# Down projection: when the weight differences are formed, when raw buffers are released, and where the third weight buffers lie

## The chip, the core and the metric

The kernel runs on one core of one Trainium2 chip. The metric is the device time of one execution in microseconds. Three runs of the kernel before gave 825.61, 826.12 and 826.38 us; their median is 826.12 us. Profiles are of one further execution, taken by the hardware profiler.

## The reference

One layer of a hybrid decoder: an attention sub-layer (two mixers, merged by gates) and a channel sub-layer, a gated MLP with a causal convolution of width 3. The change lies in the last product of the channel sub-layer, the down projection of a 512 x 2816 activation with a 2816 x 1024 weight:

```python
D_MODEL = 1024
SEQ = 512
D_FF = 2816

def conv_ffn(h, w_up, conv_w, conv_b, w_down):
    u = h @ w_up
    s = u.shape[1]
    up = jnp.pad(u, ((0, 0), (CONV_WIDTH - 1, 0), (0, 0)))
    c = conv_b + conv_w[0] * up[:, 0:s]
    for j in range(1, CONV_WIDTH):
        c = c + conv_w[j] * up[:, j:j + s]
    val, gate = jnp.split(c, 2, axis=-1)
    return (jax.nn.silu(gate) * val) @ w_down
...
        x = x + (merged @ w_out[l]).astype(x.dtype)
        h2 = rmsnorm(x, ffn_norm_g[l])
        x = x + conv_ffn(h2, w_up[l], conv_w[l], conv_b[l], w_down[l]).astype(x.dtype)
```

## The kernel before

All large products are made of float32r parts. A float32 operand x is rounded by ScalarE into a high part (`whi`) and VectorE subtracts to get a low part (`wlo = x - whi`); a product is then three matmuls: high by high, low by high, high by low.

The down projection is a 2 x 2 block product in Winograd's form with seven block products instead of eight, numbered 1 to 7. Blocks of the activation are 256 tokens by 1408 columns, blocks of the weight 1408 by 512. The 1408 rows are eleven rows of 128, taken in six chunks `CH` (two rows each, but one in the fifth). An *item* (j, c, n) is product j on the n rows from c. There are 42 items in three stretches: products 1, 5, 6 chunk by chunk (in the last chunk 1, 6, 5), then 7 and 3, then 2 and 4. One item of two rows is 12 matmuls of 512 columns: two halves of 128 tokens, each four with `whi` and two with `wlo`. The banks are `ps_a` (products 1 and 2), `ps_b` (5 and 3) and `ps_mm` (6, 7 and 4). Where a product follows another in the same bank, the sums of the first are copied out by ScalarE (`ev`) and added to by VectorE first.

The operand on the weight side is a raw block for products 1, 3 and 2, and a *difference* for the others, made by VectorE on float32 tiles of 128 x 1024:

- product 5: raw 5 less raw 1, in place;
- product 6: raw 6 less product 5's operand, into the tile T (T2 in the code);
- product 7: raw 3 less raw 7, in place;
- product 4: raw 2 less T, into T.

`load_next` (L1499) loads raw blocks of `w_down` through SP's queue into six places: three tiles `raw` and three slices of `hA`, an older buffer that the up projection's convolution uses until its end. `prepare` (L1572) makes one item ready: `weights` (L1537) forms the operand, and with it any difference, and `parts` (L1518) rounds and subtracts it. The pairs `whi`/`wlo` rotate over three buffers; every third item uses `whi3`/`wlo3`, which lie in the pool "down" together with T. This pool opens where the up projection's operands (`hh2`, `hl2`) lay. `AHEAD = 2`: item k + 2 is prepared ahead of the matmuls of item k. In the second and third stretches the activation operand of products 3 and 4 is rounded and subtracted too (`Sb`), after the weight's.

Within the down projection TensorE, VectorE and ScalarE run in the order in which the code is written (a manual schedule); SP's queue is ordered by the scheduler. The last lines of the up projection and the first item are outside of it. `users` holds for each place how many items must be ready before it is loaded again; before the change this is the number of items up to the end of the chunk, for all blocks of the chunk alike.

```python
        for k in range(len(items)):
            while len(ready) < min(k + 1 + AHEAD, len(items)):
                prepare()
            ...
            while load_next():
                pass
            product(k)
```

Of the kernel before, what the change touches and what calls it, by code (L numbers as in the profile page):

```python
# [12 lines left out]
F32 = mybir.dt.float32  # L13
F32R = mybir.dt.float32r
I32 = mybir.dt.int32
AF = mybir.ActivationFunctionType
ALU = mybir.AluOpType
# [66 lines left out]
def hybrid_block(ctx: ExitStack, tc: tile.TileContext, A: dict, out: bass.AP):  # L84
    nc = tc.nc
# [16 lines left out]
    def pool(name, side="left"):  # L102
        cm = tc.tile_pool(name=name, bufs=1, side=side)
        return cm, cm.__enter__()
# [8 lines left out]
    def mmb():  # L113
        return bank("mm", 4)
# [13 lines left out]
    def act(o, i, f=AF.Copy, **kw):  # L128
        sc.activation(o, i, f, **kw)  # L129

    def tt(o, a, b, op):
        v.tensor_tensor(o, a, b, op=op)  # L132
# [32 lines left out]
    for name in ("rwkv_mu", "rwkv_w0", "rwkv_a0", "rwkv_k_k", "rwkv_k_a", "rwkv_r_k", "rwkv_ln_g", "rwkv_ln_b"):  # L165
        r0, n = ROWS[name]
# [173 lines left out]
    with tc.manual_schedule(engines={getattr(mybir.EngineType, e) for e in ("PE", "Activation", "DVE", "Pool")}):  # L340
# [3 lines left out]
        hi = wp.tile([128, KT, 128], F32R, name="whi", tag="whi", bufs=2)  # L344
        lo = wp.tile([128, KT, 128], F32R, name="wlo", tag="wlo", bufs=2)
# [22 lines left out]
        r0, n = ROWS["rwkv_mu"]  # L368
# [45 lines left out]
    def dense_fm(xh, xl, kt=KT):  # L414
        return run(dense_fm_g(xh, xl, kt))
# [213 lines left out]
    for k in range(31):  # L629
        m, n = 31 - k, k + 1  # L630
# [7 lines left out]
    def dense_tok_g(n, xh, xl, kt=KT, halves=False, ends=False):  # L638
# [32 lines left out]
        for j, ks in enumerate(tiles[:-2]):  # L671
            parts = [(ks, wnext(len(ks), n))]
            for ts_ in ([range(2), range(2, NT)] if halves and j == 0 else [range(NT)]):
                yield from passes(parts, ts_)
# [420 lines left out]
    at_cm, at = pool("att")  # L1095
# [321 lines left out]
    with tc.manual_schedule(engines=KTS):  # L1417
        for t in range(NT):
            qs = slice(128 * t, 128 * t + 128)
            p = mmb()  # L1420
# [43 lines left out]
    def conv(p, f, i):  # L1464
        c = cgv[:, i]
        act(c, p, AF.Identity, scale=cw[:, 2, f:f + 1], bias=cw[:, 3, f:f + 1])
        stt(c[:, 1:], p[:, :-1], cw[:, 1, f:f + 1], c[:, 1:])
        stt(c[:, 2:], p[:, :-2], cw[:, 0, f:f + 1], c[:, 2:])
        return c

    def sums(i, lf, rt):
        l0, l1, r0, r1 = lf[:, 0:256], lf[:, 256:512], rt[:, 0:256], rt[:, 256:512]
        s1, s2, s3 = (tmp[:, j] for j in range(3))
        tt(s3, l0, l1, ALU.subtract)
        tt(s1, l1, r1, ALU.add)
        tt(s2, s1, l0, ALU.subtract)
        tt(s4[:, i], r0, s2, ALU.subtract)
        for w, x in zip(split, (l0, s1, s2, s3)):
            act(w[:, 0, i], x)
            tt(w[:, 1, i], x, w[:, 0, i].bitcast(F32), ALU.subtract)  # L1480
# [4 lines left out]
    def places():  # L1485
        yield from (0, 1, 2, 3)
        while True:
            yield from (0, 1, 2, 4, 5, 3)

    items, fetch = [], []  # L1490
    for js, last, froms in (((1, 5, 6), (1, 6, 5), ((1, 0, 0), (5, 0, 1), (6, 1, 1))),
                            ((7, 3), (7, 3), ((7, 0, 1), (3, 1, 1))), ((2, 4), (2, 4), ((2, 1, 0),))):
        for c, n in CH:
            items += [(j, c, n) for j in (last if c + n == NFH else js)]
            fetch += [(*f, c, n, len(items)) for f in froms]

    raws, turns3, turn, place, start, users = {}, itertools.count(), places(), [], [], [0] * 6

    def load_next():  # L1499
        if not start:  # L1500
            start.append(next(slots) % 3)
            place.append(next(turn))
        i = place[0]
        if not fetch or users[i] > len(ready) or (i > 3 and not T2):
            return False
        j, kh, fh, c, n, users[i] = fetch.pop(0)
        place[0] = next(turn)
        if i < 3:
            raw = wp.tile([128, n, 512], F32, name="raw", tag=f"raw{(start[0] + i) % 3}", bufs=1)
        else:  # L1510
            o = {3: 2048, 4: 0, 5: 1024}[i]
            raw = hA[:, o:o + 512 * n].rearrange("p (k n) -> p k n", k=n)
        r0 = 128 * (NFH * kh + c)
        nc.sync.dma_start(raw, w_down[r0:r0 + 128 * n, 512 * fh:512 * fh + 512].rearrange("(k p) n -> p k n", p=128))
        raws[j, c] = raw
        return True

    def parts(x, n):  # L1518
        if next(turns3) % 3 < 2:
            hi = wp.tile([128, n, 512], F32R, name="whi", tag="whi", bufs=2)  # L1520
            lo = wp.tile([128, n, 512], F32R, name="wlo", tag="wlo", bufs=2)
        else:
            hi, lo = (dn.tile([128, n, 512], F32R, name=k, tag=k) for k in ("whi3", "wlo3"))
        act(hi, x)
        tt(lo, x, hi.bitcast(F32), ALU.subtract)
        return hi, lo

    done = {}

    def difference(c):  # L1530
        if ("T1", c) not in done:
            x = raws[5, c]
            tt(x, x, raws[1, c], ALU.subtract)
            done["T1", c] = x
        return done["T1", c]

    def weights(j, c, n):  # L1537
        x = raws.get((j, c))
        if j == 5:
            x = difference(c)  # L1540
        elif j == 6:
            t = T2[0][:, c:c + n]
            tt(t, x, difference(c), ALU.subtract)
            x = t
        elif j == 7:
            tt(x, raws[3, c], x, ALU.subtract)
        elif j == 4:
            t = T2[0][:, c:c + n]
            tt(t, raws[2, c], t, ALU.subtract)
            x = t  # L1550
        return parts(x, n)

    turnsb = itertools.count()

    def halves_of(hi, lo, x):
        act(hi, x)
        tt(lo, x, hi.bitcast(F32), ALU.subtract)
        return hi, lo

    def operand(j, c, n):  # L1560
        if j in (1, 5, 6, 7):
            w = split[(1, 5, 6, 7).index(j)]
            return w[:, 0, c:c + n], w[:, 1, c:c + n]
        if j == 2:
            return split[0][:, 0, c:c + n], split[0][:, 1, c:c + n]
        x = s4[:, c:c + n] if j == 3 else right[:, c:c + n, 256:512]
        i = next(turnsb) % 5
        return halves_of(*(Sb[0][:, i, q, 0:256 * n].rearrange("p (k n) -> p k n", k=n) for q in range(2)), x)

    ready, T2, Sb, X1 = [], [], [], []  # L1570

    def prepare():  # L1572
        j, c, n = items[len(ready)]
        ready.append((weights(j, c, n), operand(j, c, n)))

    def spare_half(c, n):
        halves_of(split[0][:, 0, c:c + n], split[0][:, 1, c:c + n], right[:, c:c + n, 0:256])

    spent.append(load_next)
    left = None  # L1580
    for n_, f in enumerate(order):
        cg = conv(dense_fm(hh, hl) if n_ else lead[0], NF + f, n_ % 2)
        act(cg, cg, AF.Silu)
        cv = conv(dense_fm(hh, hl) if n_ else lead[1], f, 2 + n_ % 2)
        if n_ == NF - 1:
            while load_next():
                pass
            prepare()
        if n_ % 2 == 0:
            tt(cv, cv, cg, ALU.mult)  # L1590
            left = cv
        else:
            tt(right[:, f - NFH], cv, cg, ALU.mult)
            sums(f - NFH, left, right[:, f - NFH])
    close(h2_cm)
    dn_cm, dn = pool("down", "right")
    T2.append(dn.tile([128, NFH, 512], F32, name="T2"))
    dpad = dn.tile([128, 32], F32, name="dpad")
    nc.gpsimd.memset(dpad, 0.0)  # L1599

    BX, BY, BZ = [pa(), pa()], [pb(), pb()], [mmb(), mmb()]
    pbank = {1: BX, 2: BX, 5: BY, 3: BY, 6: BZ, 7: BZ, 4: BZ}
# [1 line left out]
    def add_out(t, hf, x, cs=slice(0, 512), queue=None):  # L1604
        o = X1[0][:, hf, t, cs]
        tt(o, o, x, ALU.add)
        if queue:
            queue.dma_start(out[0][128 * t:128 * t + 128, 512 * hf + cs.start:512 * hf + cs.stop], o)
# [55 lines left out]
    with tc.manual_schedule(engines=KTS | {mybir.EngineType.DVE, mybir.EngineType.Activation}):  # L1664
        for k in range(len(items)):
            while len(ready) < min(k + 1 + AHEAD, len(items)):
                prepare()
            if k >= 2:
                j, c, n = items[k - 2]
                if j == 1:  # L1670
                    spare_half(c, n)
            while load_next():
                pass
            product(k)
            if items[k][0] == 3 and items[k][1] == 0:
                for hf in (1, 0):
                    nc.sync.dma_start(X1[0][:, hf], x1d[hf])
            if items[k][0] == 3 and items[k][1] == CH[2][0]:
                for i in range(2):
                    add_out(2 + i, 1, ev[1][:, i])  # L1680
# [28 lines left out]
```

## Time and profile before

| | before |
|---|---|
| median of 3 runs | 826.12 us (825.61 to 826.38) |
| profiled execution, time | 826.63 us |
| profiled execution, span of the core | 824.9 us |
| matmuls (TensorE) | 5253, busy 807.7 us |
| VectorE, ScalarE busy | 590.5 and 428.1 us |
| GpSimd busy | 66.2 us |

Busy time of matmuls overlaps, as they are pipelined, so TensorE's 98% does not say that it streams all the time; starts and idle times in the timeline do. A row of the timeline has the start, the time from the first start to the last end, the engine, the line, the operation, output and inputs, sizes and count, and in brackets the idle time of the engine just before with what ended it. Engines: PE is TensorE's matmul, PEld its weight load, DVE VectorE, ACT ScalarE, POOL GpSimd, SP the queue of the loads. L123 and L126 are the matmul helpers, L129 the helper of ScalarE's operations and L132 of VectorE's two-operand ones, so these are told apart by the tile names. In a table of stretches a row has the stretch, its length, the busy time and number of matmuls, the granted clock, the DMA share and GB/s.

### The profile page before, as it was taken

Reading aid. Unit: us, or ns where it says so; the run is one execution under the profiler, and the core shown is the slowest. Engines: PE = TensorE matmul, PEld = TensorE weight load, DVE = VectorE, ACT = ScalarE, POOL = GpSimd, SP = SyncE. Lnnn points to the kernel's source line nnn. Section 1 sums busy time; section 2 is a strip of 40 time slices with the busy share of each in tenths; the row PEclk is TensorE's granted clock in tenths of the full one; section 3 lists DMA queues with packets and bytes.
Section 4 is the critical chain, followed back from the end, with each engine's and each line's share of the span. In section 5 each row is a group of like instructions: output and inputs, shape, how many; then the busy total and the mean of one; then the engine's idle time right before and its main releaser. Section 6 shows DMA issues by size and latency. Waiting matters only on the chain.

```text
span 824.9 us, 13527 instructions
## 1 busy us (share of the span) xinstructions
PE 807.7 (98%) x5253; PEld 653.3 (79%) x5253; DVE 590.5 (72%) x1139; ACT 428.1 (52%) x851; POOL 66.2 (8%) x99
## 2 busy tenths in 40 slices
PE   7999999999999999999999999999999999997997
PEld 6777788987787887877888988888888888775776
DVE  6478779974565778787865577766666667777785
ACT  6766655553444767786443554444444444435432
POOL 6200020140000161011000000000000000000010
PEclk9999999999999999999999999999999999999999
DMA  7422222246372320001376143233332332547521
GB/s 234 112 78 76 77 77 78 68 125 192 103 129 78 84 72 16 26 27 41 103 274 185 52 128 98 85 100 102 102 97 84 100 103 101 186 152 261 181 89 51
DMA packets 114124, 89.26 MB, mean 108 GB/s; under 512 B 4629, under 2 KB 98764, under 8 KB 113804
## 3 DMA queue, kind: packets, MB, share of 16 engines
q1 hardware_dynamic: 110416, 82.31, 33.4%
q0 software_dynamic: 2592, 3.61, 1.6%
q10 hardware_dynamic: 1052, 2.48, 0.9%
q8 instruction: 41, 0.67, 0.3%
q14 instruction: 23, 0.19, 0.1%
HBM read 82.35 MB, written 4.39 MB: 105 GB/s over the span
## 4 chain that ended last, share of the span: by engine, by line
PE 84%; DVE 9%; ACT 3%; issue 2%; DMA 1%; ACTq 0%; SPq 0%; DVEq 0%
PE ps_mm L123 70%; PE ps_a L123 5%; PE ps_b L123 2%; DVE wlo L132 2%; ACT whi L129 2%; PE ps_mm L126 2%; DVE T L132 1%; PE ps_b L126 1%; PE ps_b L1288 1%; DVE raw L132 1%; DMA xt<-in_x_dram 1%; PE ps_a L126 1%; PE ps_mm L1288 1%; DVE XP L132 1%; DVE P L1214 0%
## 5 line engine op out<-in xcount | busy, mean ns | idle before, releaser
L123 PE MATMUL ps_mm<-hh,whi 128*128 128x512 f32 (+1 forms) x624 | 242.5, 391 | 0.3 <-DVE hl L141 0.3
L123 PE MATMUL ps_mm<-hl,whi 128*128 128x512 f32 (+1 forms) x624 | 240.3, 387 | 0.0
L129 ACT ACTIVATE whi<-raw 128x1024 fp32r<-128x1024 f32 (+3 forms) x118 | 116.1, 986 | 117.3 <-PE ps_mm L123 87.2
L307 DVE TENSOR_TENSOR wlo<-raw,whi 128x1024 fp32r<-128x1024 f32 (+1 forms) x89 | 104.4, 1174 | 90.1 <-PE ps_mm L123 67.2
L123 PE MATMUL ps_mm<-hh,wlo 128*128 128x512 f32 (+1 forms) x624 | 152.1, 384 | 0.0
L123 PEld LDWEIGHTS ps_mm<-hh,whi 128*128 128x128 f32 x624 | 117.3, 188 | 27.1 <-issue 1.0
L123 PEld LDWEIGHTS ps_mm<-hl,whi 128*128 128x128 f32 x624 | 117.3, 188 | 23.0 <-issue 1.0
L123 PEld LDWEIGHTS ps_mm<-hh,wlo 128*128 128x128 f32 x624 | 115.1, 188 | 23.4
L141 DVE SCALAR_TENSOR_TENSOR hA<-ps_mm,cw,hA 128x511 f32<-128x511 f32 (+1 forms) x88 | 65.4, 746 | 1.5
L129 ACT ACTIVATE hA<-ps_mm,cw 128x512 f32<-128x512 f32 x44 | 34.2, 781 | 19.9 <-PE ps_mm L123 18.4
L129 ACT ACTIVATE P<-P,nm 128x512 f32<-128x512 f32 (+3 forms) x64 | 35.4, 554 | 11.3 <-DVE nm L1214 10.9
L129 ACT ACTIVATE hA<-hA 128x512 f32<-128x512 f32 x22 | 13.9, 633 | 43.6 <-DVE hA L141 43.5
L307 POOL TENSOR_TENSOR wlo<-raw,whi 128x512 fp32r<-128x512 f32 (+3 forms) x13 | 20.9, 1604 | 177.0 <-PE ps_mm L123 142.8
L1214 DVE CUSTOM_DVE_ANT_0 P<-ps_a,AB 128x512 f32<-128x512 f32 (+3 forms) x64 | 29.4, 485 | 1.8 <-PE ps_a L123 1.5
L129 ACT ACTIVATE whi<-T 128x1024 fp32r<-128x1024 f32 (+1 forms) x12 | 11.9, 989 | 33.7 <-DVE T L132 31.0
L132 DVE TENSOR_TENSOR wlo<-raw,whi 128x1024 fp32r<-128x1024 f32 (+1 forms) x16 | 18.3, 1155 | 10.7 <-ACT whi L129 8.1
L1599 POOL MEMSET dpad<- 128x32 f32 x1 | 0.1, 124 | 320.7 <-PE ps_mm L123 320.7
L129 ACT ACTIVATE QK<-ps_mm 128x64 f32<-128x64 f32 (+5 forms) x56 | 14.9, 308 | 17.4 <-PE ps_mm L123 17.2
L132 DVE TENSOR_TENSOR wlo<-T,whi 128x1024 fp32r<-128x1024 f32 (+1 forms) x12 | 13.6, 1136 | 12.4 <-ACT whi L129 12.4
L123 PE MATMUL ps_mm<-whi,hh 128*128 128x280 f32 (+2 forms) x72 | 22.4, 331 | 0.0
L123 PE MATMUL ps_mm<-whi,hl 128*128 128x280 f32 (+2 forms) x72 | 21.8, 323 | 0.0
L123 PE MATMUL ps_mm<-obT,whi 128*128 128x512 f32 x64 | 20.7, 399 | 0.0
(437 smaller groups left out, 1512.4 us busy)
## 6 DMA issues: line engine op xcount, KB each, us to landing
raw<-in_w_up_dram SPq DMA_DIRECT2D x44, 512.0 KB, 3.8
raw<-in_w_in_dram SPq DMA_DIRECT2D x38, 512.0 KB, 3.7
raw<-in_w_down_dram SPq DMA_DIRECT2D x18, 512.0 KB, 3.6
hA<-in_w_down_dram SPq DMA_DIRECT2D x12, 512.0 KB, 4.3
raw<-in_w_out_dram SPq DMA_DIRECT2D x8, 512.0 KB, 3.7
xt<-in_x_dram SPq DMA_DIRECT2D x4, 512.0 KB, 5.6
raw<-in_cmp_w_v_dram SPq DMA_DIRECT2D x4, 512.0 KB, 3.7
raw<-in_w_proj_b_dram SPq DMA_DIRECT2D x8, 256.0 KB, 2.6
```

The lines of the kernel that those rows point to most:

```text
L123: te.matmul(o, lhsT=l, rhs=r, start=start, stop=stop)
L126: te.matmul(o, lhsT=l, rhs=r, start=False, stop=stop, skip_group_check=True)
L129: sc.activation(o, i, f, **kw)
L132: v.tensor_tensor(o, a, b, op=op)
L141: v.scalar_tensor_tensor(o, a, s, b, op0=op0, op1=op1)
L307: low = eng.tensor_tensor(lo, raw, hi.bitcast(F32), op=ALU.subtract)
L1214: maxima.append(v.tensor_tensor_reduce(out=P[:, i], in0=o, in1=BT[:, h, 384 - 128 * qt:512], scale=-1.0, scalar=-NEG, op0=ALU.add, op1=ALU ...
L1288: te.transpose(pt[:, 128 * i:128 * i + 128], P[:, 4 * x + i, 128 * k:128 * k + 128], ident)
L1599: nc.gpsimd.memset(dpad, 0.0)
```

## The change

`weights` and its table `done` are gone. A list `summed` takes the operand of each item; the new `difference` forms the next one, and `prepare` calls it until the operands of items k and k + 1 are there, then makes the parts of item k. So each difference is issued one item ahead of the parts that read it. In the last chunk, where product 6 follows product 1, the difference of product 5 is formed with product 1. `users` now holds two counts for each load: how many items must be ready and how many operands formed, for the block itself (raw 1: until product 1's parts and product 5's difference; raw 6: until product 6's difference; and so on). `load_next` is called after every `prepare` and not once ahead of each product. `dpad`, a tile of 32 floats between T and `whi3`, and its memset on GpSimd are gone; `wlo3` is 32 floats longer instead. `whi3` and `wlo3` thereby move down by 128 bytes; T stays. `whi3` lay at 221152 and now lies at 221024, which is 1888 past a multiple of 2048, as the other `whi`, `hh2`, `hA` and the activation's parts are.

```diff
@@ -1492,16 +1492,18 @@
         for c, n in CH:
             items += [(j, c, n) for j in (last if c + n == NFH else js)]
-            fetch += [(*f, c, n, len(items)) for f in froms]
-
-    raws, turns3, turn, place, start, users = {}, itertools.count(), places(), [], [], [0] * 6
+            at = {q[0]: k for k, q in enumerate(items) if q[1] == c}
+            last_of = {1: (1, 5), 5: (5, 6), 6: (0, 6), 7: (7, 7), 3: (3, 7), 2: (2, 4)}
+            fetch += [(*f, c, n, tuple(at[q] if q else 0 for q in last_of[f[0]])) for f in froms]
+
+    raws, turns3, turn, place, start, users = {}, itertools.count(), places(), [], [], [(-1, -1)] * 6
 
     def load_next():
...
-        if not fetch or users[i] > len(ready) or (i > 3 and not T2):
+        if not fetch or len(ready) <= users[i][0] or len(summed) <= users[i][1] or (i > 3 and not T2):
             return False
@@ -1520,27 +1522,24 @@
-            hi, lo = (dn.tile([128, n, 512], F32R, name=k, tag=k) for k in ("whi3", "wlo3"))
+            hi, lo = (dn.tile([128, 1024 + p_], F32R, name=k, tag=k)[:, 0:512 * n].rearrange("p (k n) -> p k n", k=n)
+                      for k, p_ in (("whi3", 0), ("wlo3", 32)))
         act(hi, x)
         tt(lo, x, hi.bitcast(F32), ALU.subtract)
         return hi, lo
 
-    done = {}
-
-    def difference(c):
-        if ("T1", c) not in done:
-            x = raws[5, c]
-            tt(x, x, raws[1, c], ALU.subtract)
-            done["T1", c] = x
-        return done["T1", c]
-
-    def weights(j, c, n):
+    summed = []
+
+    def difference():
+        j, c, n = items[len(summed)]
         x = raws.get((j, c))
-        if j == 5:
-            x = difference(c)
-        elif j == 6:
+        if j == 1 and items[len(summed) + 1][0] == 6 or j == 5 and (5, c) not in T1:
+            T1.add((5, c))
+            y = raws[5, c]
+            tt(y, y, raws[1, c], ALU.subtract)
+        if j == 6:
             t = T2[0][:, c:c + n]
-            tt(t, x, difference(c), ALU.subtract)
+            tt(t, x, raws[5, c], ALU.subtract)
             x = t
         elif j == 7:
             tt(x, raws[3, c], x, ALU.subtract)
@@ -1548,7 +1547,9 @@
             x = t
-        return parts(x, n)
+        summed.append(x)
+
+    T1 = set()
 
     def prepare():
-        j, c, n = items[len(ready)]
-        ready.append((weights(j, c, n), operand(j, c, n)))
+        k = len(ready)
+        j, c, n = items[k]
+        while len(summed) < min(k + 2, len(items)):
+            difference()
+        ready.append((parts(summed[k], n), operand(j, c, n)))
@@ -1586,6 +1590,8 @@
             prepare()
+            while load_next():
+                pass
...
-    dpad = dn.tile([128, 32], F32, name="dpad")
-    nc.gpsimd.memset(dpad, 0.0)
...
@@ -1665,12 +1669,12 @@
             while len(ready) < min(k + 1 + AHEAD, len(items)):
                 prepare()
+                while load_next():
+                    pass
...
-            while load_next():
-                pass
             product(k)
```

What this does to the engines' orders, at three places. First VectorE at the end of the up projection; L141 is its convolution, `right` and `hB` its last sums, `T<-raw` the first chunk's difference for product 6, `raw<-raw,hA` the second chunk's for product 5, and the rows `wlo` the low parts:

```order
 L141 SCALAR_TENSOR_TENSOR hA<-ps_mm,cw,hA 128x510
+L132 TENSOR_TENSOR T_6812<-raw 128x1024
+L141 SCALAR_TENSOR_TENSOR hA<-ps_mm,cw,hA 128x511
 L132 TENSOR_TENSOR wlo<-raw,whi 128x1024
-L141 SCALAR_TENSOR_TENSOR hA<-ps_mm,cw,hA 128x511
-L132 TENSOR_TENSOR T_6809<-raw 128x1024
-L141 SCALAR_TENSOR_TENSOR hA<-ps_mm,cw,hA 128x510
+L141 SCALAR_TENSOR_TENSOR hA<-ps_mm,cw,hA 128x510
+L132 TENSOR_TENSOR wlo_6833<-T_6812,whi_6832 128x1024
 L132 TENSOR_TENSOR right<-hA 128x512
-L132 TENSOR_TENSOR wlo_6827<-T_6809,whi_6826 128x1024
+L132 TENSOR_TENSOR raw<-raw,hA 128x1024
```

The difference T now stands ahead of the second item's low part, and the second chunk's difference ahead of its first low part.

Second, VectorE from the second chunk to the third; `s_5187` is the spare activation operand, `T<-...` the difference for product 6, and `hA<-hA,raw` the one for product 5:

```order
-L132 TENSOR_TENSOR raw<-raw,hA 128x1024
+L132 TENSOR_TENSOR T_6812<-raw 128x1024
 L132 TENSOR_TENSOR wlo<-raw,whi 128x1024
 L132 TENSOR_TENSOR s_5187<-right,s_5187 128x512
-L132 TENSOR_TENSOR T_6809<-raw 128x1024
-L132 TENSOR_TENSOR wlo_6887<-T_6809,whi_6886 128x1024
+L132 TENSOR_TENSOR wlo_6890<-T_6812,whi_6889 128x1024
+L132 TENSOR_TENSOR hA<-hA,raw 128x1024
 L132 TENSOR_TENSOR wlo<-raw,whi 128x1024
-L132 TENSOR_TENSOR hA<-hA,raw 128x1024
+L132 TENSOR_TENSOR T_6812<-hA 128x1024
 L132 TENSOR_TENSOR wlo<-hA,whi 128x1024
```

Before, a difference is followed by its own low part; now the low part of the item ahead stands between them.

Third, VectorE where products 6 and 5 end and products 7 and 3 begin; `ps_mm<-ps_mm,hA` and `ps_b<-ps_b,hA` are the additions in the banks, `hA<-hA` the difference of product 7's second chunk, `Sb` the activation operand of product 3:

```order
+L132 TENSOR_TENSOR raw<-hA,raw 128x1024
 L132 TENSOR_TENSOR wlo_7095<-raw,whi_7094 128x1024
-L132 TENSOR_TENSOR raw<-hA,raw 128x1024
 L132 TENSOR_TENSOR wlo<-raw,whi 128x1024
 L132 TENSOR_TENSOR ps_mm<-ps_mm,hA 128x512 x2
+L132 TENSOR_TENSOR hA<-hA 128x1024
 L132 TENSOR_TENSOR wlo<-hA,whi 128x1024
 L132 TENSOR_TENSOR Sb<-hB,Sb 128x512
 L132 TENSOR_TENSOR s_5187<-right,s_5187 128x512
 L132 TENSOR_TENSOR ps_b<-ps_b,hA 128x512 x2
-L132 TENSOR_TENSOR hA<-hA 128x1024
```

One difference moves ahead of the last low part of product 5, the next one from behind the additions on `ps_b` to between those on `ps_mm` and product 3's low part.

The order of TensorE is the same. ScalarE's differs at one place: the second chunk's rounding for product 5 now stands ahead of the up projection's last activation parts, and one spare half ahead of the last of these. On SP a few neighbouring loads of `w_down` change places, and the load of product 7's fourth chunk now stands ahead of the first of the two read-backs of the residual (`XP<-x1d`).

## The prediction

> **What bounds the kernel now.** I read the page first, then the matmuls of the last stage by stretches, then the waits and the timeline there.
>
> ```profile
> span 824.9 us, 13527 instructions
> PE 807.7 (98%) x5253; PEld 653.3 (79%) x5253; DVE 590.5 (72%) x1139; ACT 428.1 (52%) x851; POOL 66.2 (8%) x99
> ```
>
> TensorE looks full over the whole span, but a matmul's busy time overlaps its neighbours', so I count starts. The down projection runs 42 products from 701.61 us on. A product of two chunk rows is 12 matmuls. Its cost on a TensorE that waits for nothing, from the starts of the first four products:
>
> ```profile
> 701.61 1.07 PE L123 MATMUL ps_a<-whi,s 128*128 128x512 f32 x4
> 704.33 1.07 PE L123 MATMUL ps_b<-whi,s 128*128 128x512 f32 x4
> 707.05 1.09 PE L123 MATMUL ps_mm<-whi,s 128*128 128x512 f32 x4
> 709.84 1.08 PE L123 MATMUL ps_a<-whi,s 128*128 128x512 f32 x4
> ```
>
> 704.33 - 701.61 and 707.05 - 704.33 are 2.72 us each, 0.2267 us a matmul; the third product, which reads `whi3` and `wlo3`, takes 2.79. Now the stretches (start:end, length, busy, matmuls; each count holds the one still draining at the start, except where TensorE had stood idle):
>
> ```profile
> 701.60:709.83 8.23, 8.23 (x37) 1.00 0.44 150
> 709.83:719.98 10.15, 9.24 (x37) 1.00 0.69 240
> 719.98:742.15 22.17, 21.99 (x91) 1.00 0.42 144
> 742.15:749.38 7.23, 6.08 (x25) 1.00 0.74 252
> 749.38:753.74 4.36, 2.95 (x13) 1.00 0.40 135
> 753.74:758.36 4.62, 3.01 (x12) 1.00 0.88 328
> 758.36:778.12 19.76, 19.69 (x84) 1.00 0.59 213
> 778.12:787.32 9.20, 8.87 (x37) 1.00 0.57 200
> 787.32:799.94 12.62, 11.59 (x49) 1.00 0.23 84
> 799.94:816.40 16.46, 16.46 (x73) 1.00 0.00 0
> 816.40:820.20 3.80, 3.26 (x19) 1.00 0.23 86
> ```
>
> Length less own matmuls (36, 36, 90, 24, 12, 12, 84, 36, 48, 72, and in the last 6 whole and 12 half ones) times 0.2267 is what each stretch loses: 0.07, 1.99, 1.77, 1.79, 1.64, 1.90, 0.72, 1.04, 1.74, 0.14 and, less 0.3 for the last matmul's draining, 0.78. Sum 13.6 us: all that any change of order can win here. The third buffers' rate is 0.07 us for each of 11 whole and 3 half products, 0.9 us; some 0.2 is other slow streaming; the remaining 12.5 us are waits. The granted clock (1.00) has no part in it. Who waits:
>
> ```profile
> ACT whi L129 <- DVE T L132: 31.0, 11, 4.2
> DVE wlo L132 <- ACT whi L129: 26.4, 24, 1.7
> PE ps_mm L126 <- DVE Sb L132: 1.5, 3, 0.7
> ```
>
> VectorE and ScalarE wait for each other, 24 times on one side. One chunk (three products, 8.16 us of TensorE) shows the ring:
>
> ```profile
> 714.32 1.22 DVE L132 TENSOR_TENSOR T<-raw 128x1024 f32<-128x1024 f32 x1
> 715.66 1.06 ACT L129 ACTIVATE whi<-T 128x1024 fp32r<-128x1024 f32 x1 [2.59 <-DVE T L132]
> 716.75 1.22 DVE L132 TENSOR_TENSOR wlo<-T,whi 128x1024 fp32r<-128x1024 f32 x1 [1.21 <-ACT whi L129]
> 717.89 1.22 DVE L132 TENSOR_TENSOR wlo<-raw,whi 128x1024 fp32r<-128x1024 f32 x1
> 719.02 1.22 DVE L132 TENSOR_TENSOR hA<-hA,raw 128x1024 f32<-128x1024 f32 x1
> 720.36 1.06 ACT L129 ACTIVATE whi<-hA 128x1024 fp32r<-128x1024 f32 x1 [2.69 <-DVE hA L132]
> 721.45 1.23 DVE L132 TENSOR_TENSOR wlo<-hA,whi 128x1024 fp32r<-128x1024 f32 x1 [1.21 <-ACT whi L129]
> 722.59 0.69 DVE L132 TENSOR_TENSOR s<-right,s 128x512 fp32r<-128x512 f32 x1
> 723.19 1.22 DVE L132 TENSOR_TENSOR T<-hA 128x1024 f32<-128x1024 f32 x1
> ```
>
> VectorE goes round in 723.19 - 714.32 = 8.87 us, slower than TensorE's 8.16: five operations 1.14 apart, one 0.60 apart, and twice 1.2 us in which it stands after a difference until ScalarE has rounded it. So the bound here is a two-engine chain, not an engine.
>
> **The change, part by part.** *Differences ahead.* Instruction counts on TensorE, VectorE and ScalarE are unchanged; each difference goes one product earlier, so VectorE has another operation to do while ScalarE rounds. A round without the two waits is 5 x 1.14 + 0.60 = 6.3 us, 1.9 under TensorE's 8.16. From there the gate is the buffer: three pairs, so product k + 2 may be prepared from the start of product k, 5.4 us ahead; rounding, wait and low part take 1.06 + 0.1 + 1.22 = 2.4 us. A lost round of queueing (one 1.14 and one 0.6) still fits. Later chunks of two products need 3 x 1.14 + 0.60 = 4.0 of 5.44 us. I take the waits of these stretches as gone: 1.77, 0.72, 1.04, 1.74 and 0.78, less what in them is rate.
>
> Three stretches are not steady. (a) 709.83 to 719.98, the backlog after the up projection:
>
> ```profile
> 701.84 0.12 POOL L1599 MEMSET dpad<- 128x32 f32 x1 [320.70 <-PE ps_mm L123]
> 701.88 1.23 DVE L132 TENSOR_TENSOR wlo<-raw,whi 128x1024 fp32r<-128x1024 f32 x1 [2.58 <-PE ps_mm L123]
> 712.58 1.22 DVE L132 TENSOR_TENSOR wlo<-raw,whi 128x1024 fp32r<-128x1024 f32 x1 [1.21 <-ACT whi L129]
> ```
>
> T lies where the up projection's operand lay, so the first T cannot use VectorE's 2.58 us of idleness before 701.88: it waits like the memset. The first low part comes one operation later, 703.7 to 704.9, just ahead of its first reader (the `wlo` matmuls of the second product, 0.91 after 704.33). The low part at 712.58 gets one more difference ahead of it (+1.14) and loses its wait (-1.21): 712.5, no gain, so its product keeps about 0.5 us. The next T is then done at 712.5 instead of 715.5, and the next product's 1.4 us go. Kept: 0.5 of 1.99. What hides the first T is the 0.3 us between 704.9 and that reader at 705.24; without it the second product would wait for what is missing.
>
> (b) 742.15 to 758.36, where products 1, 6 and 5 leave their banks:
>
> ```profile
> 747.29 1.06 ACT L129 ACTIVATE hA<-ps_a 128x512 f32<-128x512 f32 x2
> 752.32 1.29 DVE L132 TENSOR_TENSOR ps_mm<-ps_mm,hA 128x512 f32<-128x512 f32 x2
> 753.10 1.20 ACT L129 ACTIVATE hA<-ps_mm 128x512 f32<-128x512 f32 x2 [1.96 <-DVE ps_mm L132]
> 753.75 1.20 PE L126 MATMUL ps_mm<-whi,s 128*128 128x512 f32 x4 [1.42 <-ACT hA L129]
> 757.63 1.29 DVE L132 TENSOR_TENSOR ps_b<-ps_b,hA 128x512 f32<-128x512 f32 x2
> 758.37 1.19 PE L126 MATMUL ps_b<-whi,Sb 128*128 128x512 f32 x4 [1.61 <-DVE ps_b L132]
> ```
>
> The first 1.79 is a rounding that stood behind its difference; with the difference ahead it starts when its buffer is free, two products early, and the wait goes. For the rest I set E, the end of the last product 1, and follow the new order: copies out E + 0.25 to 1.3, rounding to 2.4, low part to 3.6, additions on ps_mm 3.6 to 4.9. TensorE opens the next product 753.75 - 752.32 = 1.43 after the additions start, E + 5.0, and is busy with products 6 and 5 until E + 5.44: the 1.64 goes. From the additions on ps_mm to those on ps_b the trace has 757.63 - 753.61 = 4.0 us; the moved difference fits there, since that piece is set by ScalarE's copies and rounding. So ps_b starts at E + 8.9, its product 0.74 later at 9.65, and the product before it ends at 8.16: 1.5 stay, 1.6 with the square operand that now stands there; at most the 1.90 of before. Kept: 1.6.
>
> *Raw buffers singly.* SP issues the same transfers; a few neighbours change places and one weight load moves ahead of the first residual read-back.
>
> ```profile
> hA<-in_w_down_dram SPq DMA_DIRECT2D x11, 512.0 KB, 4.3
> DMA to landing us min/median/max: 2.4/3.6/5.5
> ```
>
> Each load still waits for its buffer's last reader, at most one product later than before (where a low part now follows the difference) or earlier. The tightest I find is the third chunk's: by the order in (a) its buffer is free at 707.3, so it lands 4.3 later at 711.6, and is read at about 715.4. Worth 0, from -0.3 (a load that comes late once) to +0.2.
>
> *Third buffers and dpad.* The memset goes: 0.12 us on an idle engine, 0. The move by 128 bytes gives `whi3` the offset in 2048 that all other operands have. The up projection's operands reach into the same upper part of SBUF and stream at 0.2267, so the offset is the likelier cause of 2.79 than the place. Bounds 0 and 0.9; I take 0.6. The Trainium skill, "SBUF — State Buffer", section "SBUF: two separate sides", says that TensorE has ports of its own and waits for nobody, and its section on start alignment asks only for the element's size; by that this move is worth 0, and the sum would be 815.7. The trace does not agree that all buffers stream alike (2.79 against 2.72), so I don't follow it.
>
> **The sum.** 12.5 - 0.5 - 1.6 = 10.4 us of waits, plus 0.6, is 11.0. The profiled execution took 826.6 (span 824.9 and 1.7 around it): 815.6. The median shown, 826.1, stood 0.5 lower: **815.1 us**. Ends of this case: all 13.6 won, less 0.5, gives 813.0; no gain from the offset, 1.9 kept at ps_b and half of the two bank stretches kept (1.7) gives 817.7.
>
> **Rivals.** *Only the steady chunks gain.* If (a) and (b) are bound by copies and additions whoever comes first, 1.99 + 1.79 + 1.64 + 1.90 stay, and 13.6 - 7.3 - 0.4 = 5.9 us go: 820.2. For it: these are the page's one-time hand-overs, and the chain there runs through ScalarE. Against: in 742.15 to 749.38 what came last was a rounding behind its difference.
>
> *The ring is not what holds TensorE.* If buffers, not order, release the roundings, VectorE's waits only move, and nothing measurable changes: 826. Against it stand the 24 waits of 1.2 us right behind a difference, with ScalarE idle until then (2.59, 2.69).
>
> *Slower: a difference that waits for its load.* It now stands ahead of a low part whose data are there, and holds it. 17 differences could each pay; to undo 11.0 us each must lose 0.65 us more than nothing, so loads would have to land some 4.3 + 3.8 + 0.65 = 8.8 us after issue, all along. Longest seen: 5.5. If they took 10, it would be 826.1 - 11.0 + 17 x 1.9 = 847.
>
> **Chances.** The forecast 0.76 (a good third of it without a gain from the offset); only the steady chunks 0.12; ring not the cause 0.05; slower 0.04; between these 0.03. A change under 0.2% (1.65 us) can't be told from none. Faster 0.91, same 0.05, slower 0.04. The range 813.0 to 819.0 holds the forecast's ends and the part of the first rival in which one hand-over of three improves.
>
> **What would show it.** After: VectorE's waits for `whi` fall from 26.4 to under 6 us; the chunk's period on TensorE is 8.2 us; a wait of about 1.5 us stays ahead of the first ps_b product on `Sb`, and some 0.5 in the fifth product; `whi3` products start 2.72 apart; the first down matmul stays near 701.6 and the last product ends near 809. I am wrong if VectorE then waits for weight loads, if the second product waits at 705.2, or if a stretch that I called gone still starts late behind ScalarE.

## The result, and the profile after

| | before | after |
|---|---|---|
| median | 826.24 us (825.61 to 826.38, 4 runs) | 813.34 us (812.81 to 814.46, 4 runs) |
| profiled execution, time and span | 826.63, 824.9 us | 813.09, 811.4 us |
| first matmul of the down projection to its last group of matmuls | 701.61 to 819.72 us | 700.76 to 806.52 us |

The ratio is 0.9847 (95% interval 0.983 to 0.9864): 12.9 us, 1.5% faster. The forecast was 815.1, with a range of 813.0 to 819.0.

The busy times on the page of after:

```profile
PE 801.7 (99%) x5253; PEld 654.7 (81%) x5253; DVE 589.8 (73%) x1139; ACT 428.8 (53%) x851; POOL 66.1 (8%) x98
```

VectorE and ScalarE are as busy as before; only their order changed. The chain of waits that ended last shows it better. Its line by engine, from the page of before and then from that of after:

```profile
PE 84%; DVE 9%; ACT 3%; issue 2%; DMA 1%; ACTq 0%; SPq 0%; DVEq 0%
```

```profile
PE 94%; DVE 3%; ACT 1%; DMA 1%; issue 1%; POOL 0%; DVEq 0%; POOLq 0%; ACTq 0%
```

TensorE's share of the path rises by 10 points; VectorE gives up 6, ScalarE 2 and issue 1. The stretches of the down projection after, TensorE's busy time and matmuls alone (start:end, length, busy, matmuls, granted clock, DMA share, GB/s):

```profile
700.75:708.91 8.16, 8.16 (x37) 1.00 0.54 147
708.91:717.32 8.41, 8.41 (x37) 1.00 0.81 294
717.32:745.88 28.56, 28.56 (x127) 1.00 0.64 203
745.88:752.28 6.40, 5.75 (x25) 1.00 0.78 257
752.28:806.37 54.09, 54.09 (x244) 1.00 0.36 131
```

Less own matmuls (36, 36, 126, 24) times 0.2267, the first four lose 0.00, 0.25, 0.00 and 0.96 us. In the fifth every whole product starts 2.72 us after the one ahead of it, every half one 1.36. So 1.2 us are left of the 13.6 that the stage lost before, and 12.35 of the 13.5 us between the two spans are in this stage (its exact measure stands at the head of the experiments). The rest is 0.85 us ahead of it and 0.3 behind it.

The steady ring, from one difference on T to the next (rows of VectorE and ScalarE):

```profile
716.51 1.22 DVE L132 TENSOR_TENSOR T<-hA 128x1024 f32<-128x1024 f32 x1
717.65 1.22 DVE L132 TENSOR_TENSOR wlo<-hA,whi 128x1024 fp32r<-128x1024 f32 x1
717.85 1.06 ACT L129 ACTIVATE whi<-T 128x1024 fp32r<-128x1024 f32 x1 [0.69 <-DVE T L132]
718.78 0.69 DVE L132 TENSOR_TENSOR s<-right,s 128x512 fp32r<-128x512 f32 x1
719.38 1.23 DVE L132 TENSOR_TENSOR wlo<-T,whi 128x1024 fp32r<-128x1024 f32 x1
719.85 1.06 ACT L129 ACTIVATE whi<-hA 128x1024 fp32r<-128x1024 f32 x1 [0.94 <-PE ps_a L123]
720.52 1.22 DVE L132 TENSOR_TENSOR raw<-raw,hA 128x1024 f32<-128x1024 f32 x1
721.66 1.22 DVE L132 TENSOR_TENSOR wlo<-hA,whi 128x1024 fp32r<-128x1024 f32 x1
722.57 1.06 ACT L129 ACTIVATE whi<-raw 128x1024 fp32r<-128x1024 f32 x1 [1.66 <-PE ps_b L123]
722.79 1.23 DVE L132 TENSOR_TENSOR T<-raw 128x1024 f32<-128x1024 f32 x1
```

In this round VectorE needs 722.79 - 716.51 = 6.28 us and does not wait, where it took 8.87. The last two ScalarE rows show the new gate: the rounding waits for TensorE to finish with the buffer that it writes. Rows from the table of waits after, from 690 us to the end, say the same (time in all, count, longest):

```profile
DVE wlo L132 <- ACT whi L129: 13.4, 16, 2.1
ACT whi L129 <- DVE T L132: 7.5, 5, 2.9
ACT whi L129 <- PE ps_a L126: 5.9, 4, 2.1
ACT whi L129 <- PE ps_mm L126: 5.7, 4, 2.1
DVE raw L132 <- DMA raw<-in_w_down_dram: 2.3, 1, 2.3
PE ps_b L126 <- DVE ps_b L132: 0.7, 1, 0.7
```

ScalarE's waits on VectorE's T fell from 31.0 us to 7.5, and waits on TensorE took their place. VectorE still stands 13.4 us for `whi`, but TensorE hardly waits at all: the engine that is waited for has become the one that sets the pace. The one wait for a load lies at 689.87 us, ahead of the stage.

### The profile page after: what moved, and what is told of

Its sections match the earlier page's. It is cut to its first block, busy times and chain, and to the rows that moved or that the text cites. A ratio compares the mean times of both kernels' runs of the same rounds, so it can differ in the third digit from the quotient of the medians.

```text
span 811.4 us, 13524 instructions
## 1 busy us (share of the span) xinstructions
PE 801.7 (99%) x5253; PEld 654.7 (81%) x5253; DVE 589.8 (73%) x1139; ACT 428.8 (53%) x851; POOL 66.1 (8%) x98
## 4 chain that ended last, share of the span: by engine, by line
PE 94%; DVE 3%; ACT 1%; DMA 1%; issue 1%; POOL 0%; DVEq 0%; POOLq 0%; ACTq 0%
PE ps_mm L123 72%; PE ps_a L123 7%; PE ps_b L123 4%; PE ps_mm L126 3%; PE ps_b L126 2%; PE ps_a L126 2%; PE ps_b L1288 1%; DMA pra<-in_rwkv_ln_b_dram 1%; PE ps_mm L1288 1%; DVE P L1214 0%; POOL pra L170 0%; DVE P L136 0%; ACT P L129 0%; ACT whi L129 0%; PE ps_b L575 0%
## 5 line engine op out<-in xcount | busy, mean ns | idle before, releaser
L141 DVE SCALAR_TENSOR_TENSOR hA<-ps_mm,cw,hA 128x511 f32<-128x511 f32 (+1 forms) x88 | 65.4, 746 | 1.5
L1612 POOL DMA_DIRECT2D out_dram<-XP x6 | 3.3, 546 | 422.3 <-DMA raw<-in_w_down_dram 396.3
L129 ACT ACTIVATE whi<-hA 128x1024 fp32r<-128x1024 f32 (+1 forms) x14 | 13.4, 969 | 12.8 <-PE ps_mm L126 3.7
```

The lines of the kernel that those rows point to most:

```text
L141: v.scalar_tensor_tensor(o, a, s, b, op0=op0, op1=op1)
```

## The experiments

All were timed against the kernel before (medians 825.75 to 825.94 in the three series). "Stage" is the time from the first `ps_a` matmul to the start of the last group of matmuls plus the 0.23 us of its first matmul: 118.34 before, 105.99 after.

**The third buffers, undone in the changed kernel.**

```diff
-            hi, lo = (dn.tile([128, 1024 + p_], F32R, name=k, tag=k)[:, 0:512 * n].rearrange("p (k n) -> p k n", k=n)
-                      for k, p_ in (("whi3", 0), ("wlo3", 32)))
+            hi, lo = (dn.tile([128, n, 512], F32R, name=k, tag=k) for k in ("whi3", "wlo3"))
...
+    dpad = dn.tile([128, 32], F32, name="dpad")
+    nc.gpsimd.memset(dpad, 0.0)
```

> The change without the move of the third buffers: whi3 and wlo3 where they were, dpad and its memset back. Ring theory with the offset as cause of the slow third products: every third product again starts its successor 2.79 us later instead of 2.72, 0.07 us each in 11 whole and 3 half products, so 0.9 us more than the changed kernel (0.1%), some 814.2; waits as in the changed kernel. Rival, the offset is worth nothing (the third products were slow because VectorE and ScalarE were late): third products at 2.72 here too and no time lost.

Measured: 813.91 us (813.81 to 814.41), ratio 0.9858 (0.9845 to 0.9872), stage 106.87: 0.88 us longer. Starts of the third, fourth and fifth product in its timeline:

```profile
706.25 1.09 PE L123 MATMUL ps_mm<-whi,s 128*128 128x512 f32 x4
709.04 1.08 PE L123 MATMUL ps_a<-whi,s 128*128 128x512 f32 x4
711.78 1.07 PE L123 MATMUL ps_b<-whi,s 128*128 128x512 f32 x4
```

The third product takes 2.79 again, and the one behind it 2.74. The 128 bytes are worth 0.9 us here. The medians alone would not show it (this ratio's interval overlaps with that of the changed kernel); the stage does, since the changed kernel's was 105.99 us here and 105.96 when it was profiled again.

**The third buffers alone, in the kernel before.** Here only the two tiles are moved and `dpad` taken out.

> The kernel before with the third buffers moved alone. Offset theory: third products at 2.72 us, but most of them are followed by a wait for VectorE or ScalarE, so that TensorE's 0.9 us are largely eaten: 0.2 to 0.9 us faster than before, 825.3 to 826.0. If the offset were the main cause of the whole gain: near 813.3.

Measured: 825.64 us (825.24 to 827.43), ratio 1.0 (0.9991 to 1.0009), stage 118.24, 0.10 shorter. Its stretches: to the end of the eighteenth product, the two products behind it, the rest.

```profile
700.65:752.78 52.13, 48.34 (x200) 1.00 0.55 179
752.78:760.25 7.47, 5.88 (x25) 1.00 0.90 305
760.25:818.51 58.26, 56.05 (x244) 1.00 0.32 111
```

Its third products stream at 2.72, and the waits behind them are longer for it: product 3 on the chunk of one row loses 0.60 us where it lost 0.45, two products of the last stretches 0.76 and 1.06 where they lost 0.63 and 0.99. As long as the ring sets the pace, a faster TensorE only waits more. The same edit is worth 0.9 us or nothing by what bounds the stage.

**Raw buffers by chunk again, in the changed kernel.**

```diff
-            fetch += [(*f, c, n, tuple(at[q] if q else 0 for q in last_of[f[0]])) for f in froms]
+            fetch += [(*f, c, n, len(items)) for f in froms]
...
-        if not fetch or len(ready) <= users[i][0] or len(summed) <= users[i][1] or (i > 3 and not T2):
+        if not fetch or users[i] > len(ready) or (i > 3 and not T2):
```

(`load_next` is called once ahead of each product again.)

> The change without the single release: a place is loaded again only when all items of its chunk are ready, and loads are issued once ahead of each product. Ring theory: loads have microseconds to spare, so the same time as the changed kernel, 813.3 within 0.2%. Rival, earlier loads bring the gain: VectorE waits for weight loads again and several of the 12.9 us come back, 816 to 826.

Measured: 812.7 us (812.69 to 813.25), ratio 0.9844 (0.9831 to 0.9857), stage 105.96. From product to product the starts are as far apart as after, within 0.01 us. So the single release is worth nothing to the stage: with the differences ahead, VectorE waits for no load in it either way. What it is worth with the old order was not tried alone.

**Differences ahead only from the second stretch on.** The offset and the release stay as after.

```diff
-        while len(summed) < min(k + 2, len(items)):
+        while len(summed) < min(k + (2 if k >= 17 else 1), len(items)):
...
-        if j == 1 and items[len(summed) + 1][0] == 6 or j == 5 and (5, c) not in T1:
+        if j in (5, 6) and (5, c) not in T1:
```

> The change with differences ahead only from product 7's first item on; in the first stretch (products 1, 5, 6) each difference directly precedes its own parts as before. Release and offset as in the change. Ring theory: the period of 8.9 us per chunk comes back and with it the waits from 709 to 749 (about 1.4 at the sixth product, 1.6 in the steady chunks, 1.7 ahead of the last product 6, and some of the 1.6 at the bank change): 4.5 to 6.5 us slower than the changed kernel, 818 to 820. Rival, the gain comes from the two-product stretches or the bank changes alone: under 2 us slower.

**Differences ahead only in the first stretch.**

```diff
-        while len(summed) < min(k + 2, len(items)):
+        while len(summed) < min(k + (2 if k < 17 else 1), len(items)):
```

> The change with differences ahead only in the first stretch; from product 7 on each difference directly precedes its own parts. Release and offset as in the change. Ring theory: the waits of the two later stretches come back (0.4 at product 7's second item, 0.9 at its last, 0.6, 1.0 and 0.7 where TensorE waits for Sb): 3 to 4 us slower than the changed kernel, 816 to 817.5. The losses of this and of the run with the later stretches alone together make the 10.5 to 11.5 us that the order brought, if the two stretches are independent.

Measured: late only, 820.11 us (819.95 to 820.13), ratio 0.9931 (0.9916 to 0.9946), stage 112.97, 6.98 longer than after. Early only, 818.15 us (817.73 to 818.6), ratio 0.991 (0.9893 to 0.9926), stage 110.42, 4.43 longer. Both are somewhat beyond what was expected. The same three stretches as above, of late only:

```profile
700.81:751.80 50.99, 48.24 (x199) 1.00 0.53 178
751.80:759.32 7.52, 5.91 (x24) 1.00 0.90 344
759.32:813.40 54.08, 54.08 (x244) 1.00 0.35 122
```

And of early only:

```profile
700.62:745.73 45.11, 45.11 (x199) 1.00 0.64 208
745.73:752.40 6.67, 5.74 (x25) 1.00 0.78 266
752.40:810.66 58.26, 55.97 (x244) 1.00 0.35 119
```

Each loses time only where the old order stands and at the joint. With the old order throughout and the new offset (the second experiment) the rows read 52.13, 7.47 and 58.26; after they add to 45.13, 6.40 and 54.09. So the order (with the single release, worth nothing above) brings 7.0, 1.1 and 4.2 us, 12.25 in all. The two half changes lose 6.98 + 4.43 = 11.41 of it; most of the other 0.84 is the wait ahead of product 7's first item, 1.64 us in the second experiment and 0.53 in late only. Late only is beyond what was expected by the joint: there the first `ps_b` product of product 3 waits 1.91 us and not 0.82. Early only is beyond it because the later stretches alone are worth 4.2. Late only shows the old picture row by row, too: a rounding and a low part, each waiting for the other engine.

```profile
719.55 1.06 ACT L129 ACTIVATE whi<-hA 128x1024 fp32r<-128x1024 f32 x1 [2.69 <-DVE hA L132]
720.64 1.22 DVE L132 TENSOR_TENSOR wlo<-hA,whi 128x1024 fp32r<-128x1024 f32 x1 [1.21 <-ACT whi L129]
```

**One spare activation half behind the additions.** At the wait that is left, a subtraction that no product needs yet (`s<-right,s`, the last chunk's half for product 2) stands ahead of the additions on `ps_b`. This kernel moves it behind them.

```diff
-                if j == 1:
+                if j == 1 and k != 17:
                     spare_half(c, n)
             product(k)
+            if k == 17:
+                spare_half(c, n)
```

> The changed kernel with one pair of operations moved: the spare activation half of the last chunk (ScalarE 0.52, VectorE 0.60) is made after the additions on ps_b instead of ahead of them. Theory: the 0.8 us wait ahead of product 3's first item is set by the row of ScalarE and VectorE operations between the additions on ps_mm and those on ps_b, so it shrinks by 0.6 to about 0.2 us and nothing else moves: 0.6 us less TensorE time, 812.7. Rival, that wait is set by the end of product 5 on TensorE: nothing changes.

Measured: 812.66 us (812.16 to 813.58), ratio 0.9845 (0.9832 to 0.9859), stage 105.36, 0.63 shorter than after. The wait there is 0.21 us:

```profile
747.73 1.29 DVE L132 TENSOR_TENSOR ps_b<-ps_b,hA 128x512 f32<-128x512 f32 x2
748.47 1.20 PE L126 MATMUL ps_b<-whi,Sb 128*128 128x512 f32 x4
748.92 0.68 DVE L132 TENSOR_TENSOR s<-right,s 128x512 fp32r<-128x512 f32 x1
```

The median overlaps with the changed kernel's, so both were run again on one chip, side by side.

> The changed kernel itself, timed beside the next one. Both theories: 812.5 to 813.5 us, the down projection 106.0 us from its first to its last group of matmuls.

> The changed kernel with one spare activation half of the last chunk behind the additions on ps_b, again. If the wait ahead of the first ps_b product on Sb is really on the path, the stage is 0.6 us shorter (105.4) and the median 0.4 to 0.8 us under that of the changed kernel in this series. If something later takes the gain back, the stage is 106.0 again and the medians are within 0.2 us.

Measured: the changed kernel 813.18 us (812.77 to 813.52, 5 runs), ratio 0.9847 (0.9834 to 0.9861), stage 105.96; with the half moved 812.54 us (812.53 to 812.76, 4 runs), ratio 0.984 (0.9826 to 0.9853), stage 105.38. The difference is 0.64 us, and 0.58 of it stands in the stage. The five runs of the one and the four of the other do not overlap, though the two ratios' intervals do. This is the lowest median of all versions here.

**Other offsets of the third buffers.** In the changed kernel a pad of 64 or of 256 bytes stands ahead of `whi3` (the second also moves T down by 2048 bytes). The edit for 64 bytes:

```diff
-                      for k, p_ in (("whi3", 0), ("wlo3", 32)))
+                      for k, p_ in (("whi3", 0), ("wlo3", 16)))
...
+    dpad = dn.tile([128, 16], F32, name="dpad")
+    nc.gpsimd.memset(dpad, 0.0)
```

> The changed kernel with whi3 and wlo3 64 bytes higher (1952 past a multiple of 2048; the kernel before had 2016, the change has 1888). A look at the spacing of third products alone. If any offset other than the common one is slow: 2.79 us; if only an offset of 128 modulo 256 from the others is slow: 2.72.

> The changed kernel with whi3 and wlo3 256 bytes past the common offset (96 past a multiple of 2048; T lies 2048 bytes lower to make room). If any offset other than the common one is slow: third products at 2.79 us; if what counts is the offset modulo 256 bytes: 2.72.

Measured, one run each: 64 bytes 813.97 us, stage 106.97; 256 bytes 813.08 us, stage 106.0. The third, fourth and fifth product with 64 bytes:

```profile
706.12 1.10 PE L123 MATMUL ps_mm<-whi,s 128*128 128x512 f32 x4
708.88 1.09 PE L123 MATMUL ps_a<-whi,s 128*128 128x512 f32 x4
711.65 1.07 PE L123 MATMUL ps_b<-whi,s 128*128 128x512 f32 x4
```

And with 256:

```profile
706.18 1.07 PE L123 MATMUL ps_mm<-whi,s 128*128 128x512 f32 x4
708.90 1.07 PE L123 MATMUL ps_a<-whi,s 128*128 128x512 f32 x4
711.62 1.07 PE L123 MATMUL ps_b<-whi,s 128*128 128x512 f32 x4
```

With 64 bytes both products are slow, 2.76 and 2.77; with 256 both take 2.72. So the offset in 2048 does not decide, nor does T's place, nor the memset of `dpad`, which stands in the kernels with 64, 128 and 256 bytes alike. As far as these four offsets tell, the offset in 256 does (64 and 128 off are slow, 0 and 256 off fast). The two kernels of this experiment were timed once each, so only their starts are read.

## Why the prediction was right, and where it was off

**What bounds the kernel, and the differences ahead: right.** The ring was the bound. Putting the old order back costs 7.0 us in the first stretch (1.1 of it at the joint) and 4.4 in the later ones (0.3 of it there), and apart from two places the stage streams at 2.72 us a product once it is gone. The round without waits, put at 6.3 us, took 6.28. All stretches that were called gone are gone.

**(a), the backlog: right in place, 0.5 forecast, 0.24 measured.** The first T waited as said, at the end of the up projection. The rows of the fifth product after:

```profile
710.23 1.22 DVE L132 TENSOR_TENSOR T<-raw 128x1024 f32<-128x1024 f32 x1
711.37 1.22 DVE L132 TENSOR_TENSOR wlo<-raw,whi 128x1024 fp32r<-128x1024 f32 x1
712.64 0.30 PEld L123 LDWEIGHTS ps_b<-wlo,s 128*128 128x128 f32 x2 [0.36 <-DVE wlo L132]
```

TensorE still waits for this low part. The term gave 1.14 for 1.21, a low part 0.07 earlier. Counted from the stage's first matmul it came 0.36 earlier: 711.37 - 700.76 = 10.61 us behind it, and 712.58 - 701.61 = 10.97 before. Of this, 0.15 is that a wait of 1.21 followed a difference's whole 1.22 us, 712.58 - 710.15 = 2.43 in all, while two operations in a row take 2.28; the other 0.2 are smaller gaps in the backlog. TensorE reached the product 0.1 sooner, as the third product no longer ran slow, so the wait shrank by less. The 0.3 us of cover at the second product held.

**(b), the hand-over of the banks: 1.6 forecast, 0.96 measured.** Of the terms in the stage this was the most off, and it was the size. The rows after, E being 740.45:

```profile
739.29 0.60 ACT L129 ACTIVATE hA<-ps_a 128x512 f32<-128x512 f32 x1 [0.46 <-PE ps_a L123]
740.65 0.60 ACT L129 ACTIVATE hA<-ps_a 128x512 f32<-128x512 f32 x1 [0.76 <-PE ps_a L123]
741.14 1.05 ACT L129 ACTIVATE whi<-raw 128x1024 fp32r<-128x1024 f32 x1
742.23 1.23 DVE L132 TENSOR_TENSOR wlo<-raw,whi 128x1024 fp32r<-128x1024 f32 x1 [0.91 <-ACT whi L129]
743.37 1.29 DVE L132 TENSOR_TENSOR ps_mm<-ps_mm,hA 128x512 f32<-128x512 f32 x2
748.08 0.68 DVE L132 TENSOR_TENSOR s<-right,s 128x512 fp32r<-128x512 f32 x1
748.68 1.29 DVE L132 TENSOR_TENSOR ps_b<-ps_b,hA 128x512 f32<-128x512 f32 x2
749.43 1.19 PE L126 MATMUL ps_b<-whi,Sb 128*128 128x512 f32 x4 [0.66 <-DVE ps_b L132]
```

The walk had both copies of product 1 behind E, to E + 1.3. But each half of the product is copied when that half is done, and the first is out before E; the trace of before showed the two as one row only because ScalarE came late. Rounding therefore starts at E + 0.7, and the additions on `ps_mm` at E + 2.9, not 3.6. From their end to the additions on `ps_b` are 748.68 - 744.66 = 4.0 us, and the product follows 0.75 later, both as the walk had it. So 0.82 us stay there and 0.14 in the product on `Sb`. The walk also took the order of those 4.0 us as given; the spare half in it was worth 0.6 by itself.

**Raw buffers singly: 0, right.** No load came late: VectorE waits for none in the stage. The 2.3 us in the table above lie 11 us ahead of it and stand in the trace of before as well.

**The offset: 0.6 forecast, 0.9 measured.** The offset was the cause of 2.79, as taken, and the upper bound was the value. The 0.2 us that the sum called other slow streaming is gone as well; in part it was the product behind each third one, which lost 0.01 us or a little more when the offset was put back. The Trainium skill, "SBUF — State Buffer", section "SBUF: two separate sides", says that TensorE never waits for another engine there. The traces do not speak against that, since the slow rate also stands where no other engine writes a weight (last section). But a worth of 0 for the move, which the prediction drew from this and from the rule on alignment, does not follow from either: the stage differs by 0.88 us.

**The base.** The forecast took 0.5 us from the profiled execution of before. That execution was slower than all four timed ones, and 0.85 us of it lay ahead of the stage: the kernel that differs from before only in the offset starts the stage at 700.65, not 701.61. Another 0.3 us came behind the stage, which the forecast put at nothing. They go with the order: from the start of the last group of matmuls to the end of the span are 5.2 us in the three kernels with the old order in the later stretches and 4.82 to 4.85 in the others. Together that is 1.15 and not 0.5. The terms together are 0.26 for (a), 0.64 for (b), 0.5 for the offset and the other slow streaming (0.3 and 0.2) and 0.65 here, the 2.0 us between 815.1 and the profiled 813.09. All four lie on the same side, so the median came 1.8 us under the forecast and only 0.3 above the lower end of its range.

**What would show it.** The chunk's period (8.16 us), the third products (2.72) and the place of both remaining waits came as said; the first matmul (700.76) and the last product's end (near 807) were earlier by the base and the terms. Wrong was that VectorE's waits for `whi` fall under 6 us: they fell to 13.4. They were taken as a measure of the ring, but once TensorE sets the pace somebody must wait for it, and here it is ScalarE's roundings for buffers and VectorE behind them. The rival "the ring is not what holds TensorE" had this picture with no gain; what tells them apart is TensorE's own starts, not VectorE's waits. None of the three signs of being wrong came: no wait for a load, none in the second product, and no late start in a stretch that was called gone.

**The rivals.** "Only the steady chunks gain" fell: the hand-overs kept 0.96 of 5.33 us, the backlog 0.25 of 1.99. The slower one needed loads that land 8.8 us after issue, all along; the longest of `w_down` now took 7.0 us, and VectorE waited for none in the stage. (That rival counted 17 differences; the kernel forms 24, six for each of products 5, 6, 7 and 4.)

## What to carry to other kernels

Where two engines make an operand in turns (difference, rounding, low part), give the one that would wait the next item's independent step in between; the trace shows the need as equal waits right behind one kind of row on an engine that is far from full. Judge such a change by the starts on the engine that should stream, since the helpers' waits do not go away but move to buffers. When a wait is left at a hand-over, look for work in the chain ahead of it that nobody needs yet, and measure small edits of the streaming engine only when it is the bound: the same offset was worth 0.9 us with the ring gone and 0.1 with it.

## What the runs showed of the hardware

How fast TensorE streamed float32r operands here depended on where two buffers, `whi3` and `wlo3`, lay: 12 matmuls of 512 columns took 2.72 us at 0 and 256 bytes off the others' offset, 2.79 at 128 and 2.76 at 64. The product behind, whose own operands had not moved, took 2.74 at 128 and 2.77 at 64. It is TensorE's reading that is slow, and not only while other engines write weights. With the offset put back (the first experiment), the last product of the stage starts its two halves so:

```profile
804.87 1.09 PE L126 MATMUL ps_mm<-whi,Sb 128*128 128x512 f32 x4
806.26 0.64 PE L126 MATMUL ps_mm<-whi,Sb 128*128 128x256 f32 x4
```

The first half takes 1.39 us; in the changed kernel it takes 805.33 - 803.97 = 1.36. By then ScalarE has stopped, and VectorE has ended its last operand 1.1 us before and only adds results, in both kernels. What couples the two products was not tried, nor were offsets under 64 bytes. The other operands never moved, so it is open whether the distance to them counts or the buffers' own address.

A wait of TensorE costs more than its length: behind the 0.82 us ahead of 749.43, the half product that starts there takes 750.93 - 749.43 = 1.50 us instead of 1.36. Of the 0.24 us lost in the fifth product, 0.1 is the wait and the rest is such a slow restart.
